# A parallel-branch decoder step on one core: TensorE's order in the making of h written out, the last query norms in an earlier step, gate products placed behind a projection

## The chip, the core and the metric

The program runs on one of the cores of a Trainium2 chip. The core has a matrix engine (TensorE, PE in the profile; its weight loads are shown as PEld), a vector engine (VectorE, DVE), a scalar engine (ScalarE, ACT), GpSimd (POOL) and SyncE (SP), which here issues nearly all DMAs. Each engine works through its own instructions in order; they wait for each other by semaphores. The metric is the time of one execution on the device in microseconds (us).

## What is computed

One layer of a decoder trunk, for a prompt of 1024 tokens and for 8 samples of 8 tokens, which share the weights (1088 token columns in all, 1024 features):

```python
mod = jax.nn.silu(c) @ ada_w + ada_b
shift, scale, gate = jnp.split(mod, 3, axis=-1)
h = rmsnorm(x, norm_g) * (1.0 + scale[:, None]) + shift[:, None]
z = h @ w_in + b_in
a_u, a_v, a_g, b_q, b_k, b_v, b_g, c_qk, c_v, c_i, c_f, c_o, c_g, m_g = jnp.split(z, IN_OFFSETS, axis=-1)
ya = chunk_gmlp(a_u, a_v, ...) * silu(a_g)
yb = swa_branch(rmsnorm(b_q), rmsnorm(b_k), b_v, ...) * silu(b_g)     # windowed attention, 8 heads of 64
yc = mlstm_branch(c_qk, c_v, c_i, c_f, c_o, ...) * silu(c_g)
gates = sigmoid(m_g)                                                    # three gates for each channel
merged = gates_0 * (ya @ w_branch_a) + gates_1 * (yb @ w_branch_b) + gates_2 * (yc @ w_branch_c)
x_out = x + gate[:, None] * (merged @ w_out)
```

Besides x_out the caches and states of the branches are returned.

## The kernel before

**Precision and layout.** Activations and weights of the large products are split into a high part, rounded to fp32r, and a low part, what is left; each product is three matmuls (high by high, high by low, low by high). h is kept transposed: eight tiles of 128 features by 1088 columns, `hh[k]` (high) and `hlo[k]` (low, shown as hl). The 1088 columns form three chunks, `CH`: columns 0 to 383, 384 to 767 and 768 to 1087. The nine token tiles of x (`TILES`) hold 128 rows each, the last 64.

**The planner.** The program is written in one sequence. A planner then orders each engine's instructions by its own estimates of when operands come; `tc.high_priority()` moves a block ahead, `tc.issue_after(ins)` lets the instructions of a block that run on the engine of `ins` come only behind `ins` on that engine. Inside `tc.manual_schedule(engines={PE})` TensorE keeps the written order (the kernel before has this from L1326 on, through attention, gates and projections, to the end). DMAs are instructions of SP's queue, in the order that the planner gives them.

**The making of h (L304 to L428).** The loads are issued in the order of `LOADS`: token tiles x0 to x8, adaLN weights in four groups a0 to a3 of 2 MB, the first slab of w_in in two halves w0 and w1. `norm(g)` normalises three token tiles: for each ACT squares and sums it (L322), POOL raises the sum to the power -1/2 (`rsqrt`, L162 and L163), DVE scales the tile in place (L325). `mod(j)` makes the adaLN columns of features 2j and 2j+1: 32 TensorE records from a group of adaLN weights into a PSUM bank, a copy of it by ACT (L356), eight records that sum it (L363), then small DVE instructions into `modA`, `modB` (L366, L368). `hprep(k, ci)` makes feature tile k of chunk ci: three transposes by TensorE into a `pk` bank, ACT applies scale and shift (`hf`, L382), DVE rounds to `hh` (L388) and subtracts to `hlo` (L389); in chunk 2 DVE also treats the samples' columns (L385, L387). `part(k, ci, i)` adds the three matmuls of feature tile k to the product of half i of the first slab with chunk ci. A product runs over k = 0 to 7, so six accumulators are open; before, five are: three `pg` banks and two `pu` banks, and the sixth product, of half 1 with chunk 2, follows at the end (L427). The string `STEPS` gives the written order: `N0` is norm(0), `M1` mod(1), `231` hprep and part of k = 2 to 3 in chunk 1. `P` loads and splits the next slab (`load_pieces`, split by L124 on ACT and L125 on DVE), behind the last mod's instructions; `S` brings the bias columns. In this phase TensorE's order is the planner's.

**Banks.** PSUM has eight banks: three `pg`, three `pk`, two `pu`. A bank is given again once its last reader is done.

**Attention (L1330 to L1370).** Sixteen steps `Prompt(g, n)`, for two groups of heads and eight token tiles, run as a pipeline: at turn i the phase y of step i-6, v of i-5, s of i-2, p of i-4 and q of i (`PLAN`), with other products as filling between (`filler`, in the order query tiles, gmlp tiles, gate chunks). `q` transposes the query tile (`q_transpose`). At n = 0, 3 and 6 it calls `q_stats(g, n)`, which makes the norms of three token tiles: two squares (L1011) and two sums (L1012) on DVE, `rsqrt` on POOL; for the last three it also scales the samples' rows of the raw queries by DVE (L1020). At n = 7 the samples' queries are transposed too (TensorE, in order, so it waits for L1020). Ahead of q, `filler` makes sure that the query tiles that the call of that turn reads have been projected. `s` makes scores, DVE copies a masked part (L1072), `p` transposes probabilities, which DVE masks into `Pp` and `Pc`, `v` multiplies by values. In some turns (`tail`) DVE also makes sums of h tiles for later (`t_second`).

**Gates and projections (L1760 on).** For each branch n and each p of four: two gate columns by seven half products (`seven`), then `proj` twice: four products into PSUM banks, each evacuated by DVE with the gate (L1686). In the first branch each projection is followed by `gate_b(f, b)`: SP loads half a row block of the attention output (`dy`) and of its SiLU gate (`dsg`) into one staging tile (L1755, L1756), DVE multiplies (L1757), SP stores the product back (L1758). It is read when the third branch in order begins. Weight loads (L1398) are issued five items ahead (`LEAD`).

## Time and profile before

| | |
|---|---|
| median of 3 runs | 1191.07 us (1186.18, 1191.07, 1191.6) |
| the profiled execution | 1185.67 us, span of its instructions 1184.0 us |
| DMA | 129.73 MB, mean 110 GB/s |
| mean granted TensorE clock | 0.997 |
| making of h, TensorE's first to last instruction of it | 11.07 to 75.49 us |
| attention with its filling | 400 to 600 us |
| gates and projections | 600 to 1080 us |

The profile is of one execution. In lists of groups and in the timeline a row gives the engine, the line (L85 is the helper of all matmuls, L89 that of all transposes), the output and inputs by name, the shapes and the count; in the timeline it begins with start and duration in us and ends with the idle time before it and what ended that. A matmul's duration contains its passage through the array, so matmuls that follow each other overlap; what each adds is the step from start to start. In the list of waits a row says who waited for whom, for how many us in total, how many times, and the longest. A wait for several things is put down to the one that the profile shows last.

### The profile page before, as it was taken

How to read it: one execution, taken by the hardware profiler on the slowest of the kernel's cores; microseconds unless marked ns; L12 is line 12 of the kernel's file. 1: busy time of each engine (PE TensorE's matmuls, PEld its weight loads, DVE VectorE, ACT ScalarE, POOL GpSimd, SP SyncE). 2: the span in 40 equal slices, each digit the busy share in tenths (PEclk: the TensorE clock that was granted, in tenths of full speed). 3: DMA queues.
4: the chain of work that ended last, by engine and by line, in shares of the span. 5: the costliest groups of instructions: out<-in, count | busy, mean ns of one | idle time of the engine just before them, and what ended most of it. 6: DMA issues, size and time to landing. Idle time of an engine off the chain costs nothing.

```text
span 1184.0 us, 23111 instructions
## 1 busy us (share of the span) xinstructions
PE 1154.9 (98%) x8924; PEld 1108.1 (94%) x8924; DVE 777.7 (66%) x1846; ACT 489.0 (41%) x1225; POOL 81.3 (7%) x111
## 2 busy tenths in 40 slices
PE   5899999999999999989999999999999999999998
PEld 2699999999999998978998999999999999999998
DVE  3577877655468587876598973655766676668433
ACT  4543455434343368877353441423322343235100
POOL 2100011102024001110000000000000000000000
PEclk9999999999999999989999999999999999999999
DMA  9821222323222110123235256424543354465422
GB/s 309 256 73 37 76 84 64 103 64 100 90 79 75 51 54 15 55 63 96 63 95 154 55 166 190 135 76 120 162 115 109 108 166 116 130 208 177 130 90 73
DMA packets 150773, 129.73 MB, mean 110 GB/s; under 512 B 13614, under 2 KB 140214, under 8 KB 150649
## 3 DMA queue, kind: packets, MB, share of 16 engines
q1 hardware_dynamic: 142984, 118.96, 34.1%
q0 software_dynamic: 2240, 7.08, 1.7%
q10 hardware_dynamic: 5440, 2.23, 0.7%
q8 instruction: 70, 1.15, 0.4%
q14 instruction: 39, 0.31, 0.1%
HBM read 99.39 MB, written 29.82 MB: 109 GB/s over the span
## 4 chain that ended last, share of the span: by engine, by line
PE 85%; DMA 5%; DVE 4%; ACT 2%; issue 1%; SPq 1%; POOL 0%; ACTq 0%; DVEq 0%
PE pg L85 47%; PE pk L85 22%; PE pu L85 13%; PE pk L89 2%; DMA stage<-dy 2%; DMA raw<-in_w_in_dram 1%; DMA dy<-stage 1%; SPq L251 1%; ACT Sm L1080 1%; DVE hl L125 1%; PE pu L89 1%; DVE Sm L1072 0%; DVE nm L1075 0%; DVE QT L1040 0%; DVE rr L1012 0%
## 5 line engine op out<-in xcount | busy, mean ns | idle before, releaser
L85 PE MATMUL pg<-hl,hl 128*128 128x256 f32 (+3 forms) x904 | 278.5, 308 | 0.8 <-DVE hl L389 0.8
L85 PE MATMUL pg<-hh,hl 128*128 128x384 f32 (+1 forms) x912 | 238.3, 335 | 3.4 <-DVE hh L388 2.3
L85 PE MATMUL pg<-hl,hh 128*128 128x256 f32 (+1 forms) x1008 | 178.0, 283 | 0.0
L85 PEld LDWEIGHTS pg<-hl,hl 128*128 128x128 f32 x904 | 170.9, 189 | 3.9 <-DVE hl L389 1.7
L85 PEld LDWEIGHTS pg<-hh,hl 128*128 128x128 f32 x912 | 161.9, 189 | 7.8 <-DVE hh L388 3.9
L85 PEld LDWEIGHTS pg<-hl,hh 128*128 128x128 f32 x1008 | 150.8, 189 | 0.3
L1408 ACT CAST prod<-raw 128x512 fp32r<-128x512 f32 x76 | 46.8, 620 | 125.0 <-PE pk L85 51.7
L85 PE MATMUL pg<-hh,prod 128*128 128x288 f32 (+1 forms) x400 | 83.9, 289 | 0.2 <-DVE prod L1409 0.2
L85 PE MATMUL pk<-hh,prod 128*128 128x256 f32 (+1 forms) x384 | 78.1, 285 | 0.0
L1572 ACT ACTIVATE tt<-tt,bh 128x288 f32<-128x288 f32 x96 | 49.8, 522 | 47.5 <-DVE tt L1517 16.2
L1409 DVE TENSOR_TENSOR prod<-raw,prod 128x512 fp32r<-128x512 f32 x76 | 51.8, 686 | 24.2 <-ACT prod L1408 24.0
L85 PEld LDWEIGHTS pg<-hh,prod 128*128 128x128 f32 x400 | 65.8, 188 | 1.1 <-issue 0.4
L85 PEld LDWEIGHTS pk<-hh,prod 128*128 128x128 f32 x384 | 62.6, 188 | 0.8 <-DVE tt L1526 0.4
L1408 ACT CAST prod<-comb 128x512 fp32r<-128x512 f32 x60 | 36.9, 615 | 62.1 <-PE pk L85 25.5
L85 PE MATMUL pg<-yh,prod 128*128 128x288 f32 (+1 forms) x288 | 60.9, 290 | 0.0
L85 PE MATMUL pk<-yh,prod 128*128 128x256 f32 (+1 forms) x288 | 58.7, 285 | 0.0
L85 PE MATMUL pg<-hl,prod 128*128 128x288 f32 (+1 forms) x200 | 57.7, 289 | 0.0
L85 PE MATMUL pu<-hh,prod 128*128 128x288 f32 (+1 forms) x272 | 56.3, 288 | 0.0
L85 PE MATMUL pk<-tc,prod 128*128 128x256 f32 (+1 forms) x408 | 56.2, 287 | 0.0
L85 PE MATMUL pg<-tc,prod 128*128 128x288 f32 (+1 forms) x396 | 55.7, 290 | 0.0
L85 PE MATMUL pk<-hl,prod 128*128 128x256 f32 (+1 forms) x192 | 54.6, 284 | 0.0
L85 PEld LDWEIGHTS pk<-tc,prod 128*128 128x128 f32 x408 | 52.6, 188 | 1.3 <-issue 0.8
(532 smaller groups left out, 2635.8 us busy)
## 6 DMA issues: line engine op xcount, KB each, us to landing
raw<-in_w_in_dram SPq DMA_DIRECT2D x124, 256.0 KB
adaraw<-in_ada_w_dram SPq DMA_DIRECT2D x16, 512.0 KB
stage<-dy SPq DMA_DIRECT2D x24, 272.0 KB
dmg<-tt SPq DMA_DIRECT2D x44, 144.0 KB
dmg<-tt SPq DMA_DIRECT2D x44, 128.0 KB
mprev<-dmg SPq DMA_DIRECT2D x32, 144.0 KB
xt<-in_x_prompt_dram SPq DMA_DIRECT2D x8, 512.0 KB
graw<-in_ada_w_dram SPq DMA_DIRECT2D x16, 256.0 KB
```

The lines of the kernel that those rows point to most:

```text
L85: T.matmul(out, lhsT=lhsT, rhs=rhs, start=start, stop=stop)
L89: T.transpose(out, in_, ident[:k, :k])
L125: V.tensor_tensor(hl[:, 1, off:off + m], raw[:, :m], hl[:, 0, off:off + m].bitcast(F32), ALU.subtract)
L251: nc.sync.dma_start(raw.rearrange("p (k c) -> p k c", k=4), kv(ada_w[:, base:base + 256])[:, 4 * (q % 2):4 * (q % 2) + 4])
L1080: newS[0] = S.activation(Sm[:, h], Sm[:, h], AF.Exp, bias=nm[:, h:h + 1], scale=rr[:, h:h + 1], accum_out=dn[:, h:h + 1]).ins
L1408: a = S.copy(t[:, 0], x)
L1409: b = V.tensor_tensor(t[:, 1], x, t[:, 0].bitcast(F32), ALU.subtract)
L1572: S.activation(x, x, AF.Tanh, bias=bh[:, b:b + 1], scale=0.5)
```

## The change

1. In the making of h TensorE's order is written out and kept (`manual_schedule`). `mod` is cut in `mod_a` (A: the first 32 records and ACT's copy) and `mod_b` (B). In the new `STEPS` a letter and digits stand for a call: `H21` is hprep(2, 1), `G31` part(3, 1) for both halves, `G420` part(4, 2, 0) for half 0 alone.
2. The sixth product is accumulated with the others, in a `pk` bank.
3. All norms are made tile by tile (before too, by `NORM1`); those of the second and third group now come behind the latest hf on ACT and the latest hlo on DVE.
4. `P` comes behind the latest hf and hlo in place of the last mod's instructions, and is written behind H71.
5. The last q_stats of each group of heads is called at n = 5 in place of 6, with its query tiles projected by then; the norms' tile r3 has three buffers.
6. The product of gate_b comes on DVE behind the latest projection evacuation (`lastev`).

```diff
@@ -29,10 +29,12 @@
 HC = HT // 2
 CUT = ((0, 288), (288, 256))
 LEAD = 5
-NORM1 = (0, 1, 2)
 LOADS = "x0 r x1 x2 a0 w0 a1 w1 x3 x4 x5 a2 x6 x7 x8 a3 s"
 
-STEPS = "N0 M0 010 M1 230 N1 M2 450 011 231 451 N2 M3 S 670 012 671 232 452 672 P"
+STEPS = """N0 A0 B0 H00 H10 G000 G100 A1 B1 H20 H30 G200 G300 G001 G101 G201 G301
+N1 H01 H11 G01 G11 H21 H31 A2 G21 B2 G31 H40 H50 H41 G40 H51 G50 G41 N2 G51
+H02 H12 G020 H22 G120 H32 G220 H42 G320 A3 H52 G420 B3 G520 H60 G021 H70 G121 G221 H61 G321 G421 H71 P G521 S
+G60 H62 G70 H72 G61 G71 G620 G720 G621 G721"""
 
 
 @with_exitstack
@@ -325,19 +327,11 @@
             V.tensor_scalar(xt[n][:tn], xt[n][:tn], y[:tn], None, ALU.mult)
 
         def norm(g):
-            if g in NORM1:
+            with ExitStack() as after:
+                for x in ("hf", "hl") if g else ():
+                    after.enter_context(tc.issue_after(last[x].ins))
                 for n in range(3 * g, 3 * g + 3):
                     norm1(n)
-                return
-            sl = slice(3 * g, 3 * g + 3)
-            for n in range(3 * g, 3 * g + 3):
-                tn = TILES[n][1]
-                junk = st.tile([128, 1024], F32, name="junk")
-                S.activation(junk[:tn], xt[n][:tn], AF.Square, accum_out=ss[:tn, n:n + 1])
-            rsqrt(rst[:, sl], ss[:, sl], 1024)
-            for n in range(3 * g, 3 * g + 3):
-                tn = TILES[n][1]
-                V.tensor_scalar(xt[n][:tn], xt[n][:tn], rst[:tn, n:n + 1], None, ALU.mult)
 
         V.tensor_tensor(sel, ident[:, 0:9], ident[:, 32:41], ALU.add)
         for i in (64, 96):
@@ -345,7 +339,7 @@
 
         last = {}
 
-        def mod(j):
+        def mod_a(j):
             pm = pk()
             for q in range(4):
                 o = slice(256 * (q // 2), 256 * (q // 2) + 256)
@@ -354,6 +348,10 @@
                        q % 2 == 0, q % 2 == 1)
             msb = st.tile([128, 512], F32, tag="msb", bufs=2, name="msb")
             last["s"] = S.copy(msb, pm)
+            last["msb"] = msb
+
+        def mod_b(j):
+            msb = last["msb"]
             pc = pk()
             if j == 0:
                 tr(pc[:, 128:160], Ra)
@@ -379,14 +377,14 @@
                 t0, tn = TILES[3 * ci + i]
                 tr(px[:, 128 * i:128 * i + tn], xt[3 * ci + i][:tn, 128 * k:128 * k + 128])
             m = min(n, 1024 - c0)
-            S.activation(hf[:, 0:m], px[:, 0:m], AF.Identity, bias=modB[:, k, 0:1], scale=modA[:, k, 0:1])
+            last["hf"] = S.activation(hf[:, 0:m], px[:, 0:m], AF.Identity, bias=modB[:, k, 0:1], scale=modA[:, k, 0:1])
             if m < n:
                 hs = hf[:, m:n].rearrange("p (b t) -> p b t", b=8)
                 V.tensor_tensor(hs, px[:, m:n].rearrange("p (b t) -> p b t", b=8),
                                 modA[:, k, 1:9].unsqueeze(2).broadcast_to([128, 8, 8]), ALU.mult)
                 V.tensor_tensor(hs, hs, modB[:, k, 1:9].unsqueeze(2).broadcast_to([128, 8, 8]), ALU.add)
             V.tensor_copy(hh[k][:, c0:c0 + n], hf)
-            V.tensor_tensor(hlo[k][:, c0:c0 + n], hf, hh[k][:, c0:c0 + n].bitcast(F32), ALU.subtract)
+            last["hl"] = V.tensor_tensor(hlo[k][:, c0:c0 + n], hf, hh[k][:, c0:c0 + n].bitcast(F32), ALU.subtract)
             if m < n:
                 S.copy(hh[k][:, NT:1152], hlo[k][:, 1024:NT].bitcast(F32))
 
@@ -396,7 +394,7 @@
         def part(k, ci, i):
             c0, n = CH[ci]
             if (ci, i) not in acc:
-                acc[ci, i] = pg() if 2 * ci + i < 3 else pu_()
+                acc[ci, i] = (pg, pg, pg, pu_, pu_, pk)[2 * ci + i]()
             ps = acc[ci, i]
             whi, wlo = (wview(hl0, p, 128, 1024 * i) for p in range(2))
             mm(ps[:, :n], whi[:, k], hh[k][:, c0:c0 + n], k == 0, False)
@@ -405,27 +403,25 @@
             if k == 7:
                 conv_evac(xp0[i], 4 * i)(ci, c0, n, ps)
 
-        for step in STEPS.split():
+        def start_step(step):
+            d = [int(x) for x in step[1:]]
             if step == "P":
-                with tc.issue_after(last["m"].ins), tc.issue_after(last["s"].ins):
+                with tc.issue_after(last["hl"].ins), tc.issue_after(last["hf"].ins):
                     load_pieces(1, [None] * 3 + [st.tile([128, 528], F32, name="raw1")])
             elif step == "S":
                 ps = pk()
                 tr(ps[:, 0:68], R1)
                 V.tensor_copy(cols[:, 0:CADA], ps[:, 0:CADA])
                 V.tensor_copy(cols[:, CCB:100], ps[:, CADA:68])
-            elif step[0] == "N":
-                norm(int(step[1]))
-            elif step[0] == "M":
-                mod(int(step[1]))
+            elif step[0] == "G":
+                for i in d[2:] or range(2):
+                    part(d[0], d[1], i)
             else:
-                ci = int(step[2])
-                for k in range(int(step[0]), int(step[1]) + 1):
-                    hprep(k, ci)
-                    for i in range(2 if ci < 2 else 1):
-                        part(k, ci, i)
-        for k in range(8):
-            part(k, 2, 1)
+                {"N": norm, "A": mod_a, "B": mod_b, "H": hprep}[step[0]](*d)
+
+        with tc.manual_schedule(engines={mybir.EngineType.PE}):
+            for step in STEPS.split():
+                start_step(step)
 
         ps = pk()
         tr(ps[:, 128:160], R2)
@@ -1011,9 +1007,9 @@
                 V.tensor_tensor(qs, qr, qr, ALU.mult)
                 V.tensor_reduce(rr[:, :, 2 * i:2 * i + 2], qs.rearrange("p n (h d) -> p n h d", d=64), AX.X, ALU.add)
             rf = rr.rearrange("p n h -> p (n h)")
-            r3 = bt([128, 3, 4], "r3", bufs=2)
+            r3 = bt([128, 3, 4], "r3", bufs=3)
             rsqrt(r3.rearrange("p n h -> p (n h)"), rf, 64)
-            r3s[g] = r3
+            r3s[g, n0 // 3] = r3
             if n0 == 6:
                 for i in range(2):
                     qr = qraw[g][i][:64, 8].rearrange("p (h d) -> p h d", d=64)
@@ -1050,10 +1046,10 @@
             def q(self):
                 g, n = self.g, self.n
                 self.QT = q_transpose(g, n)
-                if n % 3 == 0:
+                if n in (0, 3, 5):
                     with tc.issue_after(newq[0]):
-                        q_stats(g, n)
-                self.rr = r3s[g][:, n % 3]
+                        q_stats(g, (n + 1) // 3 * 3)
+                self.rr = r3s[g, n // 3][:, n % 3]
                 if n == 7:
                     QTs[g] = q_transpose(g, 8)
 
@@ -1270,7 +1266,7 @@
 
         def a_norm():
             vr = bt([128, 9], "vr", tag="rr", bufs=2)
-            vq = bt([128, 9], "vq", tag="r3", bufs=2)
+            vq = bt([128, 9], "vq", tag="r3", bufs=3)
             V.tensor_reduce(vr, va, AX.X, ALU.add)
             rsqrt(vq, vr, 512)
             A["vq"] = vq
@@ -1357,7 +1353,7 @@
             for d, ph, share in PLAN:
                 if 0 <= i - d < len(steps):
                     if ph == "q" and i < 16:
-                        filler(0, ("q", i // 8, min(8, i % 8 // 3 * 3 + 2)))
+                        filler(0, ("q", i // 8, min(8, i % 8 // 3 * 3 + (5 if i % 8 == 5 else 2))))
                     if ph == "y" and i - d == len(steps) - 1:
                         filler(1 << 30)
                         hl = bhl[0]
@@ -1683,7 +1679,7 @@
                         prev = mp(CUT[j][1], "mprev")
                         lastm[0] = nc.sync.dma_start(prev, dmg[f, :, c]).ins
                     with tc.high_priority():
-                        V.scalar_tensor_tensor(x, x, 1.0, ps, ALU.add, ALU.mult)
+                        lastev[0] = V.scalar_tensor_tensor(x, x, 1.0, ps, ALU.add, ALU.mult).ins
                     if n:
                         V.tensor_tensor(x, x, prev, ALU.add)
                     if n == 2 and f % 4 == 3:
@@ -1693,7 +1689,7 @@
 
         items.append((prep, run))
 
-    gst = {}
+    gst, lastev = {}, [None]
 
     def gate_rows(g):
         def prep():
@@ -1754,7 +1750,8 @@
         c = slice(HT * b, HT * b + HT)
         nc.sync.dma_start(x, dy[1, f, :, c])
         nc.sync.dma_start(y, dsg[f, :, c])
-        V.tensor_tensor(x, x, y, ALU.mult)
+        with tc.issue_after(lastev[0]):
+            V.tensor_tensor(x, x, y, ALU.mult)
         nc.sync.dma_start(dy[1, f, :, c], x)
 
     for n in range(3):
```

## The prediction

> **What bounds the kernel now.** I read the page first, then who TensorE waited for.
>
> ```profile
> span 1184.0 us, 23111 instructions
> PE 1154.9 (98%) x8924; PEld 1108.1 (94%) x8924; DVE 777.7 (66%) x1846; ACT 489.0 (41%) x1225; POOL 81.3 (7%) x111
> ...
> PE pk L89 <- DVE th L307: 5.7, 1, 5.7
> PE pk L85 <- DMA adaraw<-in_ada_w_dram: 5.4, 2, 5.0
> PE pk L89 <- ACT ts L1230: 3.7, 1, 3.7
> PE pg L85 <- DVE hh L388: 2.3, 3, 1.1
> PE pk L85 <- ACT msb L356: 2.1, 3, 0.7
> ...
> PE pu L85 <- DVE tt L1518: 1.2, 1, 1.2
> PE pk L89 <- DVE qraw L1020: 1.0, 1, 1.0
> ```
>
> TensorE sets the time: 29.1 us of idleness in the span is all there is to win by order, and 10.7 us of it (5.7 + 5.0) pass before the first weights are there. The change aims at three places: the making of h (waits on L388, L356 and the DMA), the transposes of the last query tile (L1020, and the 3.7 us put down to L1230), and L1518 in the gates.
>
> **Part 1, making h by a fixed order.** The same instructions are issued; only their order and their waits change. Prices, from the timeline:
>
> ```profile
> 34.52 1.50 PE L85 MATMUL pk<-adaraw,sT 128*32 128x256 f32 x24
> 36.73 1.06 PE L85 MATMUL pk<-sel,msb 128*128 128x9 f32 x8 [0.70 <-ACT msb L356]
> 60.50 0.68 PE L85 MATMUL pg<-hh,hl 128*128 128x384 f32 x3
> 71.67 0.60 PE L85 MATMUL pu<-hh,hl 128*128 128x320 f32 x3
> 37.53 0.73 PEld L89 LDWEIGHTS pk<-ident,xt 128*128 128x128 f32 x6
> ...
> 38.34 0.67 ACT L382 ACTIVATE hf<-pk,modB,modA 128x384 f32<-128x384 f32 x1 [0.48 <-DVE modB L368]
> 39.48 0.35 DVE L388 CAST hh<-hf 128x384 fp32r<-128x384 f32 x1
> 39.87 0.56 DVE L389 TENSOR_TENSOR hl<-hf,hh 128x384 fp32r<-128x384 f32 x1
> ```
>
> A step A is 32 records, 24 of them in 1.50: 2.0 us. B is 1.0. Of three chunk-0 matmuls of 0.34 each, started within 0.68, two start-to-start steps take 0.34: 0.17 each. In chunk 2 it is (0.60 - 0.31)/2 = 0.145. A transpose is 0.73/6 = 0.12, so H is 0.36. From H's last transpose to its first product: about 0.3 to hf, 0.67, 0.35 and the hand-overs, 1.4 us; 0.6 more to the product with hl. From B's end (37.79) to hf is 0.55.
>
> A norm:
>
> ```profile
> 26.52 1.06 ACT L322 ACTIVATE junk<-xt 128x1024 f32<-128x1024 f32 x1
> 27.71 1.06 ACT L322 ACTIVATE junk<-xt 128x1024 f32<-128x1024 f32 x1
> 32.90 0.75 DVE L325 TENSOR_SCALAR xt<-xt,rstd 128x1024 f32<-128x1024 f32 x1
> ...
> 36.72 1.06 ACT L322 ACTIVATE junk<-xt 128x1024 f32<-128x1024 f32 x1
> 38.23 0.55 POOL L163 TENSOR_TENSOR rstd<-ss,mhalf 128x1 f32<-128x1 f32 x1
> 38.81 0.75 DVE L325 TENSOR_SCALAR xt<-xt,rstd 128x1024 f32<-128x1024 f32 x1 [0.24 <-POOL rstd L163]
> ```
>
> One square each 1.19 us, and from a square's start to the scaled tile 38.81 + 0.75 - 36.72 = 2.84. The new issue_after puts N1's squares behind hf of H30 and N2's behind hf of H51.
>
> Now the new order laid end to end with these prices.
>
> ```profile
> 26.68 1.06 PE L85 MATMUL pk<-sel,msb 128*128 128x9 f32 x8
> 53.43 2.23 ACT L124 CAST hl<-raw 128x528 fp32r<-128x528 f32 x4
> 58.56 0.62 PE L85 MATMUL pg<-hh,hl 128*128 128x384 f32 x2 [1.06 <-DVE hh L388]
> 75.18 0.31 PE L85 MATMUL pu<-hh,hl 128*128 128x320 f32 x1
> L85 PE MATMUL pg<-hl,hh 128*128 128x264 f32 x6 | 1.3, 284 | 0.0
> ```
>
> - A1 now stands behind the products G000 and G100. That puts B1 some 0.6 later than its 26.68: 27.3 to 28.3. hf of H20 is at 28.9, of H30 at 29.4. G200 starts at about 30.0 and eighteen products (3.1, with 0.8 of waits for hh and hl) end at 33.9.
> - N1's squares start at 29.9, the third at 32.3, its tile is scaled at 35.2; before it was at 32.90 + 0.75 = 33.65. H01 ends at 35.4, G01 starts at 36.9. TensorE has only six transposes from 33.9 on: **2.3 us idle**. A2 could fill them, but stands later in the order.
> - From 36.9: 48 products 8.2, 18 transposes 2.2, A2 2.0, B2 1.0 and about 1.5 of waits (hl of chunk 1; hh and hl of H40 behind B2) end with G51 at 51.7.
> - H51's transposes end at 48.6, hf starts at 48.8, the squares at 49.4, 50.6 and 51.8, and tile 8 is scaled at 54.6. G020 starts at 56.2. From 51.7 there are six transposes to do: **3.8 us idle**.
> - From 56.2: 48 products of chunk 2 7.0, 24 of k = 6 and 7 4.1, 30 transposes 3.6, A3 2.0, B3 1.0, S 0.1, in all 17.8, and about 3.0 of short waits where a product follows its own H by one step: it ends at 77.0.
>
> Before, the last product is at 75.18, ends at 75.3 by its step, and has among it eight products of the next slab (the six of the grouped row and two of their low part, 1.0) and four small transposes (0.3): 74.0. So part 1 costs **+3.0**. What it wins is in the sum: slab 1's splits (2.23 on ACT from 53.43) no longer stand ahead of k = 6's hh, whose wait was 1.06 at 58.56. They run after H71, near 71 to 74, and are covered by the remaining products, with 3 us to spare; were that cover gone, the next slab would start up to 3 us late. Their DMAs keep their place: the edge is on ACT and DVE alone. The sixth accumulator takes one of three pk buffers; two remain for transposes, an H gives its buffer back 0.9 us after its last transpose, and the order puts at least 0.4 of products between two H, twice that between most. I cost it at nothing, up to 0.4 at each of six places if a release is late. Bounds for part 1: without the two idle stretches (2.3 + 3.8) it is -3.1. The upper end is rival C's.
>
> **Part 2, the last query norms.** The rows of the second group, in order (the first row, a gmlp tile's, is from the first group's last steps):
>
> ```profile
> 438.36 0.27 DVE L1228 TENSOR_TENSOR vn<-pg,avb 128x128 f32<-128x128 f32 x1
> ...
> 509.16 1.03 DVE L1011 TENSOR_TENSOR qs<-qraw 128x384 f32<-128x384 f32 x2
> 511.49 2.27 POOL L163 TENSOR_TENSOR r<-rr,mhalf 128x12 f32<-128x12 f32 x1
> 512.42 0.76 DVE L1072 COPY_PREDICATED Sm<-mprv,pk 128x256 f32<-128x256 uint8 x2
> 515.64 0.48 DVE L1020 TENSOR_TENSOR qraw<-qraw,r 64x128 f32<-64x128 f32 x2
> 516.06 0.47 PE L89 MATMUL pk<-ident,qraw 64*128 64x64 f32 x2 [3.72 <-ACT ts L1230]
> ...
> 502.00:504.00 2.00, 2.00 (x20) 2.00 (x20) 1.97 (x5) 2.00 (x8) 0.00 (x0) 1.00 0.23 66
> 514.00:516.00 2.00, 0.00 (x0) 0.00 (x0) 1.94 (x7) 1.71 (x8) 0.00 (x0) 0.85 0.00 0
> 516.00:518.00 2.00, 1.94 (x7) 1.85 (x8) 1.35 (x7) 1.52 (x8) 0.21 (x1) 0.50 0.00 0
> 522.00:524.00 2.00, 2.00 (x16) 1.59 (x13) 0.42 (x1) 1.33 (x4) 0.36 (x1) 0.94 0.00 0
> ```
>
> (In a stretch: its length, then PE, PEld, DVE, ACT, POOL busy, granted clock, DMA.) The releaser named is not the one: PE transposes qraw, which L1020 scales at 515.64, after squares at 509.16 and POOL's power, 511.49 to 513.76, and then 1.9 us in DVE's queue. And the gap is followed by half clock: 0.85 in the stretch from 514 is 0.6 us at 0.50, so it falls at 515.4; 0.94 from 522 is 0.24 us, so it recovers at 522.2. TensorE worked 6.2 us at half speed: 3.1 lost. The stall cost 6.8 in all.
>
> One step earlier (some 7 us), squares come near 499 and L1020 near 504: this wait goes. Late next is L1072, which frees the bank of this transpose: it ends at 513.2, for a TensorE that is there at 512.3; with L1020's 0.48 ahead of it the rest of the wait is 1.1, too short for this fall. In return DVE gets 2.0 of sums (L1011 and L1012) and 0.5 of L1020 into a stretch where it is full (1.97 of 2.00): I take 0.7 for the products that wait for Pp and Pc there, between 0 and 2.5. So -(3.72 - 1.1) - 3.1 + 0.7 = **-5.0**. The first group's wait, 1.0 in the list, goes but for 0.1: **-0.9**. Projecting the query tiles sooner issues nothing new: filling has passed them (gmlp tiles, L1228, are written at 438), so no weight DMA moves. The third r3 buffer keeps the new group from waiting for the first one's readers. Bounds: 0 and -7.8.
>
> The Trainium skill ("TensorE: Matmul & The Clock Gate", Part 1) says that the clock halves after an idle window of 3.41 us, in windows that run free. This trace agrees: from 515.4 to 522.2 are two such windows. By that rule a rest of 1.1 us keeps the clock, which is my sum; a wait above 3.4 us would lose it again.
>
> **Part 3, gate products.**
>
> ```profile
> 731.23 0.73 DVE L1757 TENSOR_TENSOR stage<-stage 128x544 f32<-128x544 f32 x1 [4.80 <-DMA stage<-dy]
> 740.77 0.37 PE L85 MATMUL pu<-yh,prod 128*128 128x288 f32 x1 [1.16 <-DVE tt L1518]
> ```
>
> L1757 holds DVE for 4.8 us waiting for its DMA, evacuations queue behind it, and TensorE waits once, 1.16. Behind the projection's last evacuation the data is there. The store behind the product is issued later on SP, with it the next stage load and whatever weight load SP has behind them; the loads run five items ahead, which covers a few us. **-1.2**, between -1.2 and +1.2 should SP hold up one weight load as long.
>
> **Sum.** +3.0 - 0.9 - 5.0 - 1.2 = -4.1 against the profiled execution, 1185.67 (span 1184.0 and 1.67 around it): 1181.6. The four times known of this kernel are two pairs, 1185.67 and 1186.18, 1191.07 and 1191.6; the median is of the upper pair, where the same sum gives 1187.0. The new median may fall to either. I say 1184.5, between.
>
> **The rivals.**
> - B: the order pays off. N1 and N2 do not hold TensorE, because ACT and DVE come to them sooner than I lay out or the products around them are slower; the two idle stretches vanish. For it: 3.8 of mine rest on three squares in a row behind hf of H51. Against: 18 products (3.1) cannot cover a chain of 1.19 + 1.19 + 2.84. Part 1 is -3.1, the sum -10.2: 1175.5 or 1180.9.
> - C, slower: the idle stretches of 2.3 and 3.8 are long and broken only by transposes, and the clock falls in both as it did at 515.4. Price 3.1 to 3.4 each: part 1 is +9.5, the sum +2.4, 1188.1 or 1193.5. It decides where TensorE is nearly idle for the 3.1 to 3.7 us that sufficed there. For it: the second stretch lasts 4.5. Against: transposes every 1.2 us break it, and about 4 us of broken work around 56 left matmuls at full speed afterwards (0.34 at 60.50).
> - D: the change of part 2 does not do what it says, since DVE's queue and not the chain of the norm is what comes late: L1020 or L1072 still ends near 516 and the clock falls. Part 2 gives only the first 0.9; the sum is +0.9, 1186.6 or 1192.0. For it: DVE is full from 498 to 516. Against: this work moves ahead of the backlog.
>
> **How the numbers follow.** Mine 0.45, B 0.25, C 0.15, D 0.15. About 0.5% (6 us) is what a measurement of this kernel can tell from no change. Mine counts as faster at the lower level and as the same at the upper: 0.22 and 0.23. B is faster, 0.25. C is the same but for 0.06 of worse falls; D is the same: together 0.24. That gives faster 0.47, same 0.47, slower 0.06. The range from 1176.0 to 1193.0 leaves out part of B's lower level and C's upper one.
>
> **What would show it.** Step 1: squares of tiles 3 to 5 behind hf of H30, transposes of chunk 2 waiting for L325 near 52 to 55, chunk 2 ending near 77. Step 2: the two-record transpose of qraw (64x64) without a wait for L1020, no stretch at 0.50 near 516. Step 3: no L1757 idle on a DMA ahead of evacuations. I am wrong if chunk 2 ends before 74, or if a stretch at half clock stands in the first 80 us.

## The result, and the profile after

| | before | after |
|---|---|---|
| median | 1187.72 us (1186.18 to 1191.6, 10 runs) | 1195.29 us (1194.22 to 1199.82, 10 runs) |
| the profiled execution | 1185.67 us, span 1184.0 | 1197.07 us, span 1195.4 |
| mean granted clock of it | 0.997 | 0.990 |

The ratio is 1.0063, 95% interval 1.0048 to 1.0078: the change costs 7.6 us, where the forecast's sum was a gain of 4.1.

First the list of who TensorE waited for, of the kernel after. Line numbers have moved: L87 is now the matmuls' helper, L91 the transposes'.

```profile
PE pk L87 <- DMA adaraw<-in_ada_w_dram: 6.6, 4, 5.4
PE pk L91 <- DVE th L309: 5.8, 1, 5.8
PE pg L87 <- DVE hh L386: 2.9, 4, 1.0
PE pk L87 <- ACT yh L1645: 2.8, 1, 2.8
PE pk L87 <- DVE QT L1036: 2.7, 2, 1.9
PE pu L87 <- DVE hh L386: 1.8, 2, 1.1
PE pk L91 <- DVE xt L327: 1.6, 2, 1.1
...
PE pk L91 <- DVE xts L327: 1.1, 1, 1.1
PE pk L87 <- ACT msb L350: 0.7, 1, 0.7
```

Of the waits that were aimed at, L1020 (1.0), the 3.7 at qraw and L1518 (1.2) are gone and msb is shorter (2.1, now 0.7). The wait for hh, also aimed at, has grown from 2.3 to 4.7 (2.9 and 1.8; its line is now L386). And there are waits that were not there before: xt and xts in the making of h (2.7 together), QT (2.7), yh (2.8). TensorE is busy for 1162.5 us in place of 1154.9, with the same 8924 instructions: it worked slower, at a lower clock.

To place the loss, the two traces are compared at equal counts of TensorE instructions (worked out from when each starts). The kernel after is behind by 9.1 us at 107 us and by 9.6 at 455; by 12.0 at 480; by 6.6 at 538 and 6.8 at 740; by 5.4 from 754 to 843; and by 11.4 from 860 to the end, the difference of the two spans. So the making of h costs +9.1, the first group's scores +2.4, the second group's transposes return 5.4, the wait in the gates returns 1.4, and something near 850 us costs +6.0; 0.7 comes in small pieces between. (The expectations below have 5.3 and 2.6 for the second and the first group, from a coarser count.)

**Making of h.** The timeline of the kernel after, and its 2-us stretches (length, then PE, PEld, DVE, ACT and POOL busy, granted clock, DMA share, GB/s):

```profile
27.43 1.06 PE L87 MATMUL pk<-sel,msb 128*128 128x9 f32 x8 [0.71 <-ACT msb L350]
...
30.16 0.45 PE L87 MATMUL pg<-hh,hl 128*128 128x384 f32 x1 [0.97 <-DVE hh L386]
...
37.58 0.45 PE L87 MATMUL pg<-hh,hl 128*128 128x384 f32 x1 [0.83 <-DVE hh L386]
...
53.20 0.33 PE L91 MATMUL pk<-ident,xt 128*128 128x128 f32 x1 [0.43 <-DVE xt L327]
54.66 0.33 PE L91 MATMUL pk<-ident,xt 128*128 128x128 f32 x1 [1.14 <-DVE xt L327]
56.12 0.27 PE L91 MATMUL pk<-ident,xts 64*128 64x64 f32 x1 [1.13 <-DVE xts L327]
...
58.43 0.63 PE L87 MATMUL pu<-hh,hl 128*128 128x320 f32 x1 [1.15 <-DVE hh L386]
...
106.79 2.11 PE L87 MATMUL pg<-hl,hh 128*128 128x264 f32 x16
```

```profile
32.00:34.00 2.00, 2.00 (x9) 2.00 (x8) 0.94 (x2) 1.65 (x4) 1.55 (x4) 0.62 1.10 359
34.00:36.00 2.00, 2.00 (x8) 1.78 (x7) 1.28 (x2) 0.00 (x0) 1.16 (x2) 0.52 1.05 409
...
52.00:54.00 2.00, 1.09 (x6) 0.58 (x4) 0.90 (x2) 1.77 (x4) 1.47 (x4) 1.00 1.24 395
54.00:56.00 2.00, 0.33 (x1) 0.14 (x1) 1.28 (x2) 0.00 (x0) 1.20 (x2) 1.00 0.44 185
56.00:58.00 2.00, 1.16 (x4) 0.57 (x4) 0.60 (x4) 1.13 (x2) 0.00 (x0) 0.60 0.16 66
58.00:60.00 2.00, 1.57 (x5) 1.17 (x5) 1.64 (x6) 0.49 (x2) 0.00 (x0) 0.50 0.00 0
...
66.00:68.00 2.00, 2.00 (x30) 0.91 (x22) 0.58 (x2) 0.30 (x2) 0.00 (x0) 0.84 0.00 0
```

The waits stand where the new order was laid out: chunk 1 starts at 37.58, chunk 2's transposes come one by one as L327 scales their tiles, one each 1.46 us. But the clock is at half from 32.5 to 35.9 and again from 56.4 to 66.6; the timeline's last row holds the last 16 products of the next slab's first grouped run, which end at 106.79 + 2.11 = 108.90; before, the same row started at 97.74 (`pg<-hl,hh`, 16 records) and ended at 97.74 + 2.11 = 99.85. This is called the slab's end below.

How much of that is waiting and how much is the clock can be read in one row: PE's busy time from 11 us to that slab's end, 592 records in both kernels (a stretch of PE alone: its bounds, length, PE busy, granted clock, DMA share, GB/s). First the kernel before, then after:

```profile
11.00:99.85 88.85, 81.49 (x592) 1.00 0.59 183
```

```profile
11.00:108.90 97.90, 86.70 (x592) 0.93 0.54 167
```

Idle is the length less the busy time: 88.85 - 81.49 = 7.4 before, 97.90 - 86.70 = 11.2 after. So +9.05 is 3.8 of more idleness and 5.2 of the same work done more slowly. (0.4 of the idleness lies ahead of the new order: TensorE's first adaLN product starts at 11.47 in place of 11.07. From a stretch's clock the moment of a fall is worked out: 0.75 in the one from 32 to 33 us is 0.5 us at half speed, so it falls at 32.5.)

**Attention and gates.** The kernel after: two timeline rows at QT with the stretches around the first, then the product that waits for yh, SP's rows for the tile `stage` ahead of it, and the clock there.

```profile
461.73 0.73 PE L87 MATMUL pk<-KT,QT 128*128 128x256 f32 x4 [1.85 <-DVE QT L1036]
...
529.43 0.72 PE L87 MATMUL pk<-KT,QT 128*128 128x256 f32 x4 [0.88 <-DVE QT L1036]
...
849.12 0.61 PE L87 MATMUL pk<-yh,prod 128*128 128x288 f32 x1 [2.79 <-ACT yh L1645]
```

```profile
460.00:462.00 2.00, 0.27 (x2) 0.30 (x3) 1.17 (x5) 1.95 (x11) 0.00 (x0) 1.00 0.00 0
462.00:464.00 2.00, 2.00 (x14) 2.00 (x13) 0.45 (x1) 2.00 (x9) 0.00 (x0) 0.64 0.23 66
464.00:466.00 2.00, 2.00 (x12) 2.00 (x11) 0.81 (x2) 1.12 (x4) 0.00 (x0) 0.50 0.00 0
...
846.00:850.00 4.00, 1.06 (x5) 0.51 (x3) 3.28 (x6) 3.56 (x8) 0.00 (x0) 0.79 0.39 125
850.00:854.00 4.00, 4.00 (x18) 4.00 (x19) 2.31 (x6) 0.52 (x2) 0.00 (x0) 0.50 0.47 139
```

```profile
826.07 0.32 SPq L1755 DMA_DIRECT2D dy<-stage  x1
826.44 0.43 SPq L1644 DMA_DIRECT2D stage<-dy  x1
...
844.22 5.95 SPq L1644 DMA_DIRECT2D stage<-dy  x3
```

The scores wait for a bank that the copies of QT have not left yet: 1.85 us, and then 3.4 us at half clock. In the gates the last product leaves `stage` at 826.07 (L1755 is the store). Only behind it come the loads of the next branch's operand (L1644, in `y_load`), which go through the same tile; the last are issued at 844.22, a projection waits 2.79 for them, and half clock follows.

### The profile page after: what moved, and what is told of

The parts are those of the page before. It is cut to its first block, busy times and chain, and to the rows that moved or that the text cites. A ratio compares the mean times of both kernels' runs of the same rounds, so it can differ in the third digit from the quotient of the medians.

```text
span 1195.4 us, 23121 instructions
## 1 busy us (share of the span) xinstructions
PE 1162.5 (97%) x8924; PEld 1115.3 (93%) x8924; DVE 780.1 (65%) x1846; ACT 488.4 (41%) x1225; POOL 82.0 (7%) x111
## 3 DMA queue, kind: packets, MB, share of 16 engines
q8 instruction: 70, 1.15, 0.4%
## 4 chain that ended last, share of the span: by engine, by line
PE 91%; DVE 2%; DMA 2%; ACT 1%; issue 1%; POOL 0%; ACTq 0%; DVEq 0%; POOLq 0%; SPq 0%
PE pg L87 49%; PE pk L87 24%; PE pu L87 14%; PE pk L91 2%; DMA raw<-in_w_in_dram 1%; PE pu L91 1%; DMA E<-scr 1%; DMA stage<-dy 0%; ACT Sm L1076 0%; DVE hl L127 0%; DVE QT L1036 0%; DVE hl L387 0%; ACT hf L380 0%; POOL r L165 0%; ACT hl L126 0%
## 5 line engine op out<-in xcount | busy, mean ns | idle before, releaser
L87 PE MATMUL pg<-hl,hl 128*128 128x256 f32 (+3 forms) x904 | 278.9, 308 | 0.6
L87 PE MATMUL pg<-hh,hl 128*128 128x384 f32 (+1 forms) x912 | 238.8, 336 | 2.9 <-DVE hh L386 2.9
L87 PE MATMUL pg<-hl,hh 128*128 128x256 f32 (+1 forms) x1008 | 179.3, 285 | 0.0
L87 PEld LDWEIGHTS pg<-hl,hl 128*128 128x128 f32 x904 | 171.4, 190 | 2.8 <-DVE hl L387 2.0
L87 PEld LDWEIGHTS pg<-hh,hl 128*128 128x128 f32 x912 | 162.4, 190 | 6.6 <-DVE hh L386 4.4
L87 PEld LDWEIGHTS pg<-hl,hh 128*128 128x128 f32 x1008 | 151.9, 190 | 0.3
L87 PE MATMUL pg<-hh,prod 128*128 128x288 f32 (+1 forms) x400 | 83.9, 289 | 0.2 <-DVE prod L1405 0.2
L87 PE MATMUL pk<-hh,prod 128*128 128x256 f32 (+1 forms) x384 | 78.1, 285 | 0.0
L1404 ACT CAST prod<-comb 128x512 fp32r<-128x512 f32 x60 | 36.9, 616 | 73.9 <-PE pk L87 30.3
L87 PEld LDWEIGHTS pg<-hh,prod 128*128 128x128 f32 x400 | 65.8, 188 | 1.1 <-DVE prod L1405 0.4
L87 PEld LDWEIGHTS pk<-hh,prod 128*128 128x128 f32 x384 | 62.6, 188 | 0.8 <-issue 0.4
L87 PE MATMUL pk<-yh,prod 128*128 128x256 f32 (+1 forms) x288 | 59.3, 286 | 2.8 <-ACT yh L1645 2.8
L87 PE MATMUL pg<-yh,prod 128*128 128x288 f32 (+1 forms) x288 | 61.7, 293 | 0.0
L87 PE MATMUL pg<-hl,prod 128*128 128x288 f32 (+1 forms) x200 | 57.7, 289 | 0.0
L87 PE MATMUL pu<-hh,prod 128*128 128x288 f32 (+1 forms) x272 | 56.3, 288 | 0.0
L87 PE MATMUL pk<-tc,prod 128*128 128x256 f32 (+1 forms) x408 | 56.2, 287 | 0.0
L87 PE MATMUL pg<-tc,prod 128*128 128x288 f32 (+1 forms) x396 | 55.7, 290 | 0.0
L87 PE MATMUL pk<-hl,prod 128*128 128x256 f32 (+1 forms) x192 | 54.6, 284 | 0.0
L87 PEld LDWEIGHTS pk<-tc,prod 128*128 128x128 f32 x408 | 52.6, 188 | 1.3 <-issue 1.3
```

The costliest lines, as they stand in the source:

```text
L87: T.matmul(out, lhsT=lhsT, rhs=rhs, start=start, stop=stop)
L1404: a = S.copy(t[:, 0], x)
```

## The experiments

Each kernel is compared with the kernel before in runs on the same chip; "by" is the difference of the medians, with the ratio's 95% interval. "Part 1 alone" and so on are the parts of the change as the prediction numbers them.

**Each part by itself.** The edit of the first three is that part of the diff, applied to the kernel before.

> The kernel before with part 1 alone (the written order of the making of h, the sixth accumulator, norms behind hf and hl). Theory: part 1 carries most of the loss; its waits for the norms cost about 3 us and two falls of the granted clock near 32 and 56 us some 6 more, so the slab's last matmul comes 9 us later than before and the time is 6 to 10 us above before. Rival 1, waits only (the falls are chance): the last matmul comes about 3 us later and no stretch near 56 us is below clock 1.00. Rival 2, the loss is made elsewhere by parts 2 and 3: within 2 us of before.

Measured: 1196.57 against 1189.59, by +7.0, ratio 1.0052 (1.0036 to 1.0069).

```profile
11.00:108.64 97.64, 86.53 (x592) 0.93 0.55 168
```

The slab ends at 108.64, with 11.1 us idle and 86.5 busy, and the clock is at half from 32.1 to 35.6 and from 56.0 to 66.3: all as in the kernel after. Part 1 carries the loss.

> The kernel before with part 2 alone (the last query norms at n = 5). Theory: the wait of 3.72 at 516 us and its clock fall go (-5.3), but the scores of the first group of heads wait about 1.8 for the copy of QT near 450 us and the clock falls there (+2.6): the time is 2 to 4 us below before. Rival 1, as forecast: -5.9. Rival 2, the new wait is a consequence of the shift by part 1: no wait for QT above 0.5 and -5 to -6.

Measured: 1185.66 against 1189.59, by -3.9, ratio 0.9972 (0.9957 to 0.9987). From the timeline, and then two stretches behind it (PE alone):

```profile
453.33 0.71 PE L85 MATMUL pk<-KT,QT 128*128 128x256 f32 x4 [1.92 <-DVE QT L1040]
```

```profile
454.00:456.00 2.00, 2.00 (x14) 0.66 0.23 66
456.00:458.00 2.00, 2.00 (x12) 0.50 0.00 0
```

The new wait belongs to part 2 itself, not to the shift by part 1.

> The kernel before with part 3 alone (gate products behind a projection's evacuation). Theory: the wait of 1.16 near 740 us goes, but the gate products are spread until 817 us, the loads of the next branch's operand use the same staging tile and start only then, and the first projection of that branch waits 2 to 3 us for them with a clock fall after it: +3 to +5 against before. Rival 1, as forecast: -1.2. Rival 2, the late loads cost only their wait, without a fall: +1 to +2.

Measured: 1193.7 against 1189.59, by +4.1, ratio 1.0033 (1.0017 to 1.0049). Its list of waits has

```profile
PE pk L85 <- ACT yh L1649: 3.1, 1, 3.1
```

and no row of L1518; half clock follows from 849.4 to 856.2. The three parts add up: 7.0 - 3.9 + 4.1 = +7.2 against +7.6 measured for all.

The same parts of this kernel that the change doesn't touch gave a surprise. Its making of h has TensorE's order of the kernel before, instruction by instruction, and yet its slab ends at 106.39, not at 99.85:

```profile
11.00:106.39 95.39, 88.84 (x592) 0.86 0.57 172
```

Idle is 6.6, no more than before, but busy is 7.4 more: the clock is at half from 20.0 to 33.6, from 40.5 to 47.3 and from 60.9 to 67.8. Seven profiled executions have this order:

| kernel | slab's end, us | PE busy from 11 us | idle | mean clock in it |
|---|---|---|---|---|
| before | 99.85 | 81.49 | 7.4 | 1.00 |
| part 2 alone | 100.61 | 81.73 | 7.9 | 1.00 |
| part 3 alone | 106.39 | 88.84 | 6.6 | 0.86 |
| early gate products (next) | 103.63 | 84.36 | 8.3 | 0.96 |
| part 2, QT first | 104.08 | 84.25 | 8.8 | 0.93 |
| part 2, early gates | 101.25 | 81.53 | 8.7 | 1.00 |
| parts 2 and 3 mended | 104.26 | 85.26 | 8.0 | 0.91 |
| mean | 102.87 | 83.92 | 7.9 | |

Against this mean the two executions with part 1's order (108.90 and 108.64, busy 86.70 and 86.53) end 5.9 later: 3.2 more idle and 2.7 more busy. The first adaLN product starts at 11.70 in the mean of the seven and at 11.47 and 11.37 in the two, so from that product on they are idle for 3.5 more and end 6.2 later. The profiled execution of before is one of three without a fall in this phase, and the best of seven.

Two executions are few to price the clock with. The mean granted clocks of all executions on the chip that ran part 1 alone tell the kernels apart less: 0.9918 over its six, 0.9922 over 29 of the kernel before (0.988 to 0.997). The difference, 0.0004 of 1190 us, is 0.5 us. By this count the kernel before spends nearly as much time at half clock, though not at the same places in each execution.

**The gates: where the product stands, or the tile it holds.**

```diff
-                if n == 0:
-                    items.append(act(gate_b, (p, i)))
+                if n == 0 and p < 2:
+                    items.append(act(gate_b, (2 * p + i, 0), (2 * p + i, 1)))
```

> As the kernel with part 3 alone, but the eight gate products are written two behind each of the first four projections, in place of one behind each of the eight. Theory: the staging tile is free by about 755 us, the first two loads of the next branch's operand are in it long before it is needed, so the wait near 840 us and its clock fall go and only the gain is left: -2 to 0 against before, 4 to 6 below part 3 alone. Rival (the products' place behind the evacuations is itself what costs): within 1.5 us of part 3 alone.

Measured: 1188.3 against 1189.59, by -1.3, ratio 0.999 (0.9974 to 1.0006), and 5.4 below part 3 alone. SP's rows for `stage`:

```profile
771.77 0.34 SPq L1759 DMA_DIRECT2D dy<-stage  x1
772.16 0.43 SPq L1648 DMA_DIRECT2D stage<-dy  x1
774.62 0.32 SPq L1648 DMA_DIRECT2D stage<-dy  x1
821.81 0.32 SPq L1648 DMA_DIRECT2D stage<-dy  x1
```

The tile is free at 772 (755 was expected), the first two loads are in it, and the third follows when the first branch's last product has let go of yh. From 740 to 900 TensorE is never idle and the clock stays at 1.00. The products still stand behind evacuations; it was the tile that cost. The -1.3 itself is within what these runs can tell from nothing.

**The making of h: waits or clock.** The next kernel keeps order and waits, and gives TensorE unread products to do while it waits.

```diff
-STEPS = """N0 A0 B0 H00 H10 G000 G100 A1 B1 H20 H30 G200 G300 G001 G101 G201 G301
-N1 H01 H11 G01 G11 H21 H31 A2 G21 B2 G31 H40 H50 H41 G40 H51 G50 G41 N2 G51
-H02 H12 G020
+STEPS = """N0 A0 B0 H00 H10 G000 G100 A1 D4 B1 H20 H30 D5 G200 G300 G001 G101 G201 G301
+N1 D12 H014 H11 D4 G01 G11 H21 H31 A2 G21 B2 G31 H40 H50 H41 G40 H51 G50 G41 N2 G51
+D4 H026 H12 D6 G020
```

(`D4` is four products; the third digit of `H014` is the number behind each of its first two transposes.)

> Part 1 alone with the same order and the same waits, but TensorE gets 55 extra 128x384 products into an unread bank in the places where it waits (4 before B1, 5 after H30, 12 before H01, 4 behind each of its first two transposes, 4 after H11; 4 before H02, 6 behind each of its first two transposes, 6 after H12); nothing of the result changes. Theory: the falls near 32 and 56 us come from these waits; with the waits filled the clock stays at 1.00 and the slab's last matmul, at 106.5 in part 1 alone, comes at 99 to 102, the time falls 3 to 6 us below part 1 alone. Rival 1, the clock falls for another reason: falls at the same places, and the time as part 1 alone or up to 2 above. Rival 2, the loss is in the order and its waits and the clock adds nothing on average: no falls, yet within 1.5 us of part 1 alone.

Measured: 1194.38 against 1188.22, by +6.2, ratio 1.0059 (1.0041 to 1.0078).

```profile
11.00:110.18 99.18, 93.04 (x647) 0.98 0.54 165
```

The falls at 32 and 56 are gone; one of 3.4 us came at 71 instead. Idle is down to 6.1, but the 55 products, each 0.17 from start to start, are 9.4 us of work for 5.0 us of idleness: I had filled more than the waits, above all at N1. The run shows that busy windows keep the clock up, and that a clock of 1.00 up to 70 us does not bring the time back as long as TensorE is held (if by fillings) for as long. It does not price the falls. What came is rival 2's sign: no falls at the two places, and a time only 0.8 below part 1 alone (6.2 against 7.0), where 3 to 6 was the theory.

> Part 1 alone with two entries of the written order moved: N1 from behind G301 to before H20, and N2 from behind G41 to behind B2, so that the norms' squares hang behind hf of H10 and of H31 in place of H30 and H51. Theory: the loss of part 1 is TensorE waiting for late norms, with the falls that these waits cause; the waits for xt at 53 to 56 go, no fall near 56, the last 128x320 product comes at 76 to 80 in place of 85.4, and the time is 4 to 8 us below part 1 alone. Rival 1, the written order loses in other places (products that follow their own H too closely): less than 2 us below part 1 alone. Rival 2, the squares now wait for x in ACT's queue and hold up hf of H20: a new wait of 1 to 3 us near 26 to 30 and less than 3 us gained.

```diff
-... A1 B1 H20 H30 ...
-N1 H01 H11 ... B2 G31 ... G41 N2 G51
+... A1 B1 N1 H20 H30 ...
+H01 H11 ... B2 N2 G31 ... G41 G51
```

Measured: 1194.34 against 1188.22, by +6.1, ratio 1.0047 (1.003 to 1.0065). From its timeline:

```profile
29.42 1.06 PE L87 MATMUL pk<-sel,msb 128*128 128x9 f32 x8 [2.25 <-ACT msb L350]
33.59 0.69 PE L87 MATMUL pg<-hh,hl 128*128 128x384 f32 x1 [1.76 <-DVE hh L386]
```

Both moves work against each other. N2 no longer holds chunk 2 (no wait for xt, no fall near 56), but N1's squares now stand in ACT's queue ahead of the copy of msb and of hf, and TensorE waits 4.0 us there: rival 2, though it is msb as well as hf that is late. So N2 was moved alone:

> Part 1 alone with one entry of the order moved: N2 from behind G41 to behind B2 (its squares behind hf of H31 in place of H51); N1 stays. In part 1 alone TensorE is idle 11.1 us between 11 us and the slab's end at 108.6 and busy 86.5; in the kernel before 7.4 and 81.5. Theory: the waits for xt at 53 to 56 (2.7 us) and the fall from 56 to 66 us behind them go; the fall near 32 stays: idle 8 to 9, busy 83 to 84, slab's end at 102 to 104, time 4 to 6 us below part 1 alone. Rival (the short waits behind each H in chunk 2, hidden until now by the half clock, take their place and cause a fall of their own): slab's end above 105, time less than 3 us below part 1 alone.

Measured: 1192.61 against 1189.27, by +3.3, ratio 1.0028 (1.0013 to 1.0043): 3.6 less loss than part 1 alone, on another chip; the two intervals just overlap.

```profile
11.00:106.75 95.75, 86.06 (x592) 0.95 0.57 172
```

Idle is 9.7 (11.1 in part 1 alone), where the theory had 8 to 9, and busy is 86.06, not 83 to 84: in this execution the clock fell at 30.7 and, behind the short waits for hh in chunk 2, from 58 to 64.8. The time, 3.6 below part 1 alone, lies between the theory (4 to 6) and the rival (less than 3); the slab's end (106.75) is the rival's. A second execution with this order, the last run below, is like it: its slab ends at 106.78 with 86.91 busy, and the clock is at half from 30.1 to 36.9 and from 57.4 to 64.2.

The last on this point takes that kernel and fills four waits only as long as they are (`D4` before B1, `D5` after H30, `D4` after H11 and after H12: 17 products, not the 21 that the expectation says).

> As the run before, with 21 extra unread 128x384 products in four places (4 before B1, 5 after H30, 4 after H11, 4 after H12, the last with 4 more of waiting left), as long as the waits for msb and hh there. Theory: no window is idle enough any more, the clock stays at 1.00 up to 60 us, the slab's end is 1 to 2 us earlier than in the run before. Rival: the fall near 32 us has another cause than these waits and stays, or the norms of N1, until now hidden by it, become the wait; slab's end no earlier.

Measured: 1191.88 against 1189.27, by +2.6, ratio 1.0024 (1.0011 to 1.0037).

```profile
11.00:106.09 95.09, 87.26 (x609) 0.98 0.56 171
```

The clock stays at 1.00 until 67.8, where it falls for 3.4 us, and the end is only 0.7 sooner. The 17 extra products in the trace are 2.9 us, so without them TensorE is held for 95.09 - 87.26 + 2.9 = 10.7, against 7.4 in the profile of before: waits of 3.4 us are left that no clock explains. Over twelve executions each, the fillings raised the mean granted clock from 0.992 to 0.995, and the time fell by 0.7. From the first adaLN product on (10.94 here, 11.48 in the run before), idleness and fillings together are 10.7 against 9.2, so an estimate of what the falls that went were worth is 0.7 + 1.5, some 2 us.

**Part 2 and the whole, mended.** ACT's copies of QT stand behind exponentials; in the next kernel those of n = 7 and of the samples are placed ahead.

```diff
-                S.copy(hi, src)
-                newq[0] = V.tensor_tensor(lo, src, hi.bitcast(F32), ALU.subtract).ins
+                with tc.high_priority() if n >= 7 else ExitStack():
+                    S.copy(hi, src)
+                    newq[0] = V.tensor_tensor(lo, src, hi.bitcast(F32), ALU.subtract).ins
```

> Part 2 alone, with the copies of QT out of its bank placed ahead (high priority) for n = 7 and the samples, where the scores waited 1.92 at 453 us. Theory: the bank is late because ACT's copy stands behind exponentials; with the copy ahead the wait and the fall behind it go, 2 to 3 us below part 2 alone. Rival 1, the bank would be late anyway by the samples' chain of norms: within 1 us of part 2 alone. Rival 2, the exponentials that are now behind the copies make the probabilities late: a new wait at Sm or Pp and up to 2 us above part 2 alone.

Measured: 1183.78 against 1188.22, by -4.4, ratio 0.996 (0.9943 to 0.9977).

```profile
455.65 0.71 PE L85 MATMUL pk<-KT,QT 128*128 128x256 f32 x4 [1.02 <-DVE QT L1041]
```

The wait is halved and no fall follows, for the first of the two copies now stands behind two exponentials in place of four, the second still behind eight. By the medians it is 0.5 better than part 2 alone, which is rival 1's size and not the theory's 2 to 3; the intervals overlap, so what the copies' place is worth is not settled.

> Part 2 and the gate products two behind each of the first four projections, without part 1. If the parts add: part 2 measured -3.9 us by the medians (1185.66 against 1189.59) and the early gate products -1.3, so -4.5 to -6 against before, some 1184.5. Rival, the parts do not add (the making of h differs from run to run by more than they gain): -2 to -4.

Measured: 1183.08 against 1188.22, by -5.1, ratio 0.9954 (0.9936 to 0.9971). The parts add. Here QT was waited for 1.72 us, and the clock did not fall.

> Without part 1: part 2 with the copies of QT ahead, and the gate products two behind each of the first four projections. If they add: part 2 with QT ahead -4.4, early gate products -1.3 against before, so -5 to -6.5, near 1183. Rival (no further gain over part 2 with QT ahead): -4 to -5.

Measured: 1181.76 against 1189.27, by -7.5, ratio 0.9934 (0.9915 to 0.9954), more than the 5 to 6.5 expected, which the interval still touches. This is the best of the study, ahead of the kernel before and of the change.

> The same with the written order of the making of h, N2 behind B2. If the order is then as good as the planner's: within 1.5 us of the kernel without part 1. If it still costs: 2 to 5 us above that kernel. If it wins: more than 2 below.

Measured: 1186.92 against 1189.27, by -2.3, ratio 0.9978 (0.9963 to 0.9993): 5.2 above the same kernel without the written order. With the last norms sooner too, that order still costs (3.3 when it stands alone).

## Why the prediction was wrong

**Part 1.** The sum, +3.0, came near in size for what it counted, idle stretches: from the first adaLN product on, idleness rose by 3.4 (profile against profile) or 3.5 (against the mean of seven). The second stretch is as laid, 3.8, and measured 3.9 (0.43, 1.14, 1.13 and 1.15). The first was laid at 2.3 and measured 0.8, because the products ahead of it ran late and slowly, and waits for hh made up the rest: that the total agrees is partly luck. The step that failed is the one after it: that the work itself would run at full speed. The clock fell twice, as rival C had it, but only the second fall stands in C's stretch. The first, at 32.5, came ahead of the stretch that had been laid from 33.9 on, behind the waits for msb (0.7 at 27.4) and hh (1.0 at 30.2); in both runs that filled these it is gone. The prediction's own sign of being wrong, half clock in the first 80 us, is there. What was set against C, that broken work around 56 us had left the matmuls at full speed, came from a single execution. Six others with the same order show that this phase loses between 0 and 7.4 us of busy time to the clock, from one execution to the next.

So a second step failed with it: the sum was made against an execution without any fall there. The prediction saw two levels of the time before, some 5 us apart; the 29 executions on the chip that ran part 1 alone fill the range from 1186.45 to 1193.89 without two levels, so the two pairs were chance. Against the mean of seven part 1 costs 3.5 of waits and, by two executions, 2.7 of clock, 6.2; the medians say 7.0. By the mean granted clocks of all executions the clock's part is only some 0.5. How much of the 7.0 is clock stays open between the two; the waits are in both profiles.

The order also moves the splits of the next slab behind H71, and adds the sixth accumulator in a pk bank. Neither was tried by itself. Moving N2 takes back 3.6 of 7.0 by the medians; what the rest is, beyond waits for hh that no longer lie beside other work, is open.

**Part 2.** For the second group the forecast (-5.0) was right in size: the wait at qraw and its fall are gone, and 5.4 returned. The wait that is left is 0.88 with no fall, near the 1.1 forecast, but it is the scores waiting for QT and not the transpose waiting for L1072. The step that failed is "The first group's wait, 1.0 in the list, goes but for 0.1". The wait moved from L1020 to QT, grew to 1.85 and took the clock down with it: +2.4. I had looked for what is late next on DVE (L1072, Pp, Pc), and it came on ACT: the samples' transposes no longer wait, but ACT empties banks in its own order, behind exponentials that wait for DVE (1.60 at 447.19 in part 2 alone). The 0.7 for Pp and Pc was not seen as a wait. By the medians part 2 gives -3.9 in place of -5.9.

**Part 3.** The gain was right (1.4 where 1.2 was forecast). The step that failed is "with it the next stage load and whatever weight load SP has behind them; the loads run five items ahead". I followed the queue and not the tile. `stage` has a next user, `y_load`, whose first loads were issued at 740 us before and sat ready:

```profile
740.31 3.76 SPq L1648 DMA_DIRECT2D stage<-dy  x2
...
817.83 1.20 ACT L1649 CAST yh<-stage 128x544 fp32r<-128x544 f32 x2 [4.26 <-PE pu L85]
```

(Rows of the kernel before.) Eight loads go through two places in `stage`, one behind the other, from 818 on; with the first two only issued at 826 the chain ends too late. +4.1 in place of -1.2; the bounds of 1.2 on either side were too narrow, since they priced a weight load and nothing longer. The kernel with early products confirms it by removing it.

**The cases.** The slower outcome was tied to C alone and to the clock. The result is falls of the clock in part 1 together with failures in parts 2 and 3 that no rival named. By the medians of the parts the sum (-4.1) missed by 4.0 in part 1, 2.0 in part 2 and 5.3 in part 3, which add.

## What to carry to other kernels

When an instruction is moved later, look up who next uses each tile and bank that it holds, not only what stands behind it in its queues: both new waits, QT's bank and `stage`, were such. Before an edit is priced against one profiled execution, see how the mean granted clock differs among several executions of the same kernel; a stretch with short gaps may run at full clock in one and at half in the next. An order written by hand must carry the work of every engine that feeds it: here a norm hung behind the latest hf put 2.7 us of waits on TensorE, and hung behind an earlier hf it held up ACT's copies and, through them, TensorE for 4.0.

## What the runs showed of the clock

The half-clock stretches come on a grid. In the kernel after the first lasts from 32.5 to 35.9, 3.4 us, and the second from 56.4 to 66.6, 10.2 us; their starts lie 23.9 us apart, that is seven times 3.41. Where the grid stands differs from run to run: the first falls of the kernels with an unfilled written order start at 32.5, 32.1, 30.4, 30.7 and 30.1.

The Trainium skill ("TensorE: Matmul & The Clock Gate", Part 1) gives such free-running windows of about 3.4 us, and the trace agrees. It also says that the clock falls after an idle window and returns after a busy one. There the runs differ, and the measurement decides. One idle gap of 1.92 us (453.33) and one of 1.85 us (461.73) were enough for a fall, with TensorE at work on both sides; gaps of 1.72, 1.40 and 1.02 at the same place, and one of 0.88 in the second group, brought none. And in the kernel after the clock came back only at 66.6, though PE's records fill the stretch 60 to 66 without a gap.

Nor does the busy share in the records decide it alone. In the kernel with early gate products, where the first fall, at 58.2, gives the place of the grid, TensorE is busy for 2.12 of the 3.41 us from 34.3 to 37.7, and no fall follows; it is busy for 2.52 of those from 54.8 to 58.2, and one does. What the clock counts as work was not found out here.
